# Two-layer diffusion backbone on one core: rows finished in whole pieces on VectorE, a gate applied at the PSUM exit, and a new order at the start of the experts

## The chip, the cores and the metric

The kernel runs on one core of a Trainium2 chip, with its engines TensorE (PE), VectorE (DVE), ScalarE (ACT), GpSimd (POOL) and SyncE (SP, which mostly issues DMAs). The metric is the device time of one execution in microseconds.

## The reference

512 latent tokens and 256 context tokens of width 1024 go through two layers. In layer 0 the mixer is neighbourhood attention beside grouped-query attention and all 768 tokens are carried on; in layer 1 it is a bidirectional RWKV-7 beside a bidirectional mLSTM, and only the 512 latent tokens leave it. After each mixer comes the same tail. What is computed there, cut to one stream:

```python
m = mixer(h)                                            # per layer
x = layer_norm(DN_ALPHA * x + g1 * (m @ mix_w_out[i]), ln_g[i, 0], ln_b[i, 0])
tokens = x * (1.0 + sc2) + sh2
scores = sigmoid(tokens @ router_w)
idx = top_k(scores + router_b, 6)                       # 6 of 64 experts
gates = 2.5 * scores[idx] / sum(scores[idx])
y = sum(gates * swiglu(tokens, w1[idx], w3[idx], w2[idx])) + swiglu(tokens, sw1, sw3, sw2)
x = layer_norm(DN_ALPHA * x + g2 * y, ln_g[i, 1], ln_b[i, 1])
```

`g1`, `sc2`, `sh2` and `g2` are vectors of 1024 that come from the conditioning; layer 0 has one set for the latent and one for the context tokens, layer 1 one set.

## The kernel before

**Tiles and stages.** Tokens lie in tiles of 128 rows by 1024 columns, six in layer 0 and four in layer 1. Each layer is a mixer (0 to 517 us of the profiled execution for attention, 1400 to 2160 for the recurrent one) and then `layer_tail`, which has four parts.

**First half of the tail.** `block` projects a tile (a product in fp32 is three matmuls of high and low parts, L414 to L416), leaves PSUM through DVE with the gate g1 (L1078) and adds the old row with its sum (L1079). `first_norm` then takes mean and variance in `spread` (ACT at L878 to L880, two short DVE operations at L881 and L882). It makes the router's input h by two DVE operations over the whole tile (L1087, L1088). The normalised row x itself, which stays in `x1` as the residual, is made by one ACT pass (L1089) and two POOL passes, times `ra` and plus `rb` (L1090, L1091). `route` works on the tile before: PE transposes h (L903), multiplies by the router (L955), ACT takes the sigmoid (L961), DVE finds the six experts and writes a 0/1 `mask` (L962 to L969), PE counts ranks with a triangular matrix (L973, L974), DVE makes `cat` (L976 to L979), PE turns it (L983).

**Start of the experts.** Ranks and gates are permuted on PE (L1166). `gates` (L932 to L936) splits the gates on DVE into bf16 parts `aux`. `slots` finds with DVE comparisons (`oh`, L1179) and small matmuls (L1184) which token sits in which slot of each unit. A unit is a set of up to 128 slots of one to four experts. `fetch` gathers the rows of a unit by an indirect DMA that POOL issues (L1207); `columns_of` turns them on PE (L1258) and leaves PSUM half by ACT and half by DVE (L1260, L1261).

**Experts.** For each unit: `up` (L1217), SwiGLU (ACT L1427, DVE L1432, transposes L1233), and `down`, whose result leaves PSUM in halves, by ACT (L1247) and DVE (L1248), as `ye`. POOL issues an indirect DMA that adds it to a DRAM buffer `acc` (L1249). Expert weights come as 1 MB thirds through a ring of ten buffers `ew`, loaded by SP (L998). 49 units run in layer 0 and 37 in layer 1. A shared expert is spread between them; its result is multiplied by g2 at the PSUM exit (L1311) and added to x by POOL (L1312). Bookkeeping for experts with more than 128 tokens (`ov`, `oc`, `blk`, L1363 to L1383) feeds a loop (L1386) that runs zero times with these inputs.

**Tail end.** `acc` is loaded back as two halves per tile (L1410). For each tile the halves are added (L1415) and multiplied by g2 (L1416), 512 columns on DVE and 512 on POOL; DVE adds the row to x with its sum (L1417); `spread` again; ACT normalises (L1419). In layer 0 `done` is `keep`, which stores the row. In layer 1 it is `store`: final gain and bias, 640 columns on DVE and 384 on POOL (L2417, L2418), and the output DMA (L2419).

**What sets the order.** The program is written in one sequence, and a scheduler that simulates engine times puts each engine's instructions in order before the run; `tc.issue_after(x)` keeps what is inside behind instruction x. A change in one operation's engine or length can therefore move others on all engines. Each engine then runs its own list in order.

Of the kernel before, what the change touches and what calls it, by code (L numbers as in the profile page):

```python
# [12 lines left out]
F32 = mybir.dt.float32  # L13
# [4 lines left out]
OP = mybir.AluOpType  # L18
# [337 lines left out]
class Kern:  # L356
# [530 lines left out]
    def layer_tail(self, layer, mT, x_rows, finish, part=None, done=None):  # L887
# [7 lines left out]
        with ExitStack() as es:  # L895
# [34 lines left out]
            def gates(dst, src, rest):  # L930
# [5 lines left out]
                nc.vector.tensor_copy(dst[:, :, :, 5], rest)  # L936
# [86 lines left out]
            with ExitStack() as es2:  # L1023
# [58 lines left out]
                def first_norm(t):  # L1082
# [6 lines left out]
                    nc.scalar.activation(x, x, AF.Identity, bias=both, scale=over)  # L1089
                    nc.gpsimd.tensor_tensor(x, x, ra, op=OP.mult)  # L1090
                    nc.gpsimd.tensor_tensor(x, x, rbb, op=OP.add)  # L1091
# [43 lines left out]
            def sort():  # L1135
# [33 lines left out]
                gates(aux, pq[:, :, 1], gq)  # L1169
# [68 lines left out]
            def down(hT, parts, ws, idx):  # L1238
# [8 lines left out]
                nc.scalar.copy(y[:, 0:512], py[:, 0:512])  # L1247
                nc.vector.tensor_copy(y[:, 512:], py[:, 512:])  # L1248
# [4 lines left out]
            def columns_of(xg):  # L1253
# [3 lines left out]
                for k in range(KT):  # L1257
                    nc.tensor.transpose(p[:, k], xg[:, k * 128:(k + 1) * 128], self.k_ident[:n, :n])  # L1258
                out = wp.tile([128, KT, 128], F32, name="xT", tag="xT", bufs=2)[:, :, :n]
                nc.scalar.copy(out[:, 0:4], p[:, 0:4])  # L1260
                nc.vector.tensor_copy(out[:, 4:8], p[:, 4:8])  # L1261
# [64 lines left out]
            while loaded < 5:  # L1326
                q, k = order[loaded]
                thirds[q, k], which[q] = routed_third(q, k)
                loaded += 1
            xgs[0] = fetch(slot_of(0)[0])  # L1330
            xgs[1] = fetch(slot_of(1)[0])
            sort()
            load()
            xgs[2] = fetch(slot_of(2)[0])
            xT = columns_of(xgs.pop(0))
            done_, begin = 0, 8
            for n, u in enumerate(units):
# [12 lines left out]
                if n == 6:  # L1350
# [32 lines left out]
            nc.vector.tensor_copy(blk[:, 128:129], cum[0:1, NE - 1:NE])  # L1383
            n_more = nc.values_load(blk[0:1, 128:129], min_val=0, max_val=127)
# [1055 lines left out]
```

## Time and profile before

| | us |
|---|---|
| median of 3 runs | 2927.14 (2916.27 to 2935.19) |
| profiled execution, its own time | 2924.99 |
| its span, first to last instruction | 2923.0 |
| PE busy | 2418.9 (83%) |
| DVE busy | 1214.3 (42%) |
| ACT busy | 737.1 (25%) |
| POOL busy | 760.8 (26%) |
| mean granted TensorE clock | 0.898 |

The shares are means over stages with different limits: PE is busy nearly throughout the experts and idle in the two tail ends. So the stages are read one by one. A group of instructions is told by its line; DVE's idle time before a group, and what ended it, says which engine it waited for. A bracket in a timeline, as [3.01 <-DVE mask L969], is the idle time of that engine just before the instruction, and what ended it.

### The profile page before, as it was taken

The numbers are of one execution on the slowest core, as the hardware profiler recorded it, in microseconds if no ns is written. First come the engines' busy times: TensorE is split into PE (matmuls) and PEld (weight loads), VectorE is DVE, ScalarE is ACT, GpSimd is POOL, SyncE is SP. The second block draws the span as 40 slices with busy tenths as digits, with TensorE's granted clock in tenths as the row PEclk, the third lists the DMA queues.
The fourth block names the chain that finished last, engine by engine and source line by source line (L and its number), as shares of the span: only waits on it lengthen the run. The fifth ranks groups of instructions, "written<-read, shape, count | busy, mean of one in ns | idle before, by whom it ended". The sixth has DMA issues, their size and how long they took to land. (4 is left out here: it accounts for less than half of the span.)

```text
span 2923.0 us, 45988 instructions
## 1 busy us (share of the span) xinstructions
PE 2418.9 (83%) x18007; PEld 1469.8 (50%) x18007; DVE 1214.3 (42%) x2595; ACT 737.1 (25%) x1605; POOL 760.8 (26%) x674
## 2 busy tenths in 40 slices
PE   7789895969989999994799778866866988979981
PEld 6658664854434444331578666756755333324330
DVE  5742544473212222213753577856566212111114
ACT  3442443231101111111554443413222101111102
POOL 0111011121112222214344354434622111111114
PEclk9899997879999999997899787879976999999995
DMA  8644445658999999996224445589635999999993
GB/s 315 213 127 124 111 132 99 236 199 313 377 343 327 359 332 347 378 343 197 86 71 111 132 126 153 145 238 299 241 129 214 383 378 354 358 393 353 353 378 115
DMA packets 254089, 722.31 MB, mean 247 GB/s; under 512 B 111096, under 2 KB 137464, under 8 KB 194736
## 3 DMA queue, kind: packets, MB, share of 16 engines
q1 hardware_dynamic: 216656, 631.86, 59.2%
q0 software_dynamic: 26560, 68.09, 9.3%
q10 hardware_dynamic: 10656, 19.40, 2.1%
q8 instruction: 143, 2.34, 0.4%
q14 instruction: 74, 0.61, 0.1%
HBM read 636.45 MB, written 107.33 MB: 254 GB/s over the span
## 5 line engine op out<-in xcount | busy, mean ns | idle before, releaser
L1217 PE MATMUL pb<-ew,xT 128*32 128x512 f32 (+2 forms) x3504 | 658.6, 605 | 24.4 <-DMA ew<-in_moe_w_dram 15.4
L1217 PEld LDWEIGHTS pb<-ew,xT 128*32 128x32 f32 (+2 forms) x3504 | 210.5, 127 | 397.3 <-issue 353.9
L1217 PE MATMUL pp<-ew,hT 128*32 128x512 f32 (+2 forms) x1752 | 327.2, 603 | 7.7 <-DMA ew<-in_moe_w_dram 5.2
L1432 DVE SCALAR_TENSOR_TENSOR hs<-s,gate,pb 128x256 f32<-128x256 f32 x86 | 41.3, 480 | 649.7 <-ACT s L1427 633.9
L1207 POOL DMA_INDIRECT xg<-rows,idx x86 | 88.8, 1032 | 649.4 <-PE pp L1258 276.0
L1427 ACT ACTIVATE s<-pb 128x256 f32<-128x256 f32 x96 | 36.1, 383 | 769.9 <-PE pb L1217 746.7
L1249 POOL DMA_INDIRECT acc<-ye,idx x86 | 137.0, 1593 | 323.9 <-DMA acc<-ye,idx 146.8
L1217 PEld LDWEIGHTS pp<-ew,hT 128*32 128x32 f32 (+2 forms) x1752 | 101.6, 126 | 189.1 <-issue 175.0
L414 PE MATMUL pp<-h_hi,w_hi 128*128 128x512 f32 (+1 forms) x432 | 162.5, 377 | 8.7 <-DVE mT L389 4.3
L415 PE MATMUL pp<-h_lo,w_hi 128*128 128x512 f32 (+1 forms) x432 | 159.7, 370 | 1.0 <-DVE h_lo L410 1.0
L416 PE MATMUL pp<-h_hi,w_lo 128*128 128x512 f32 (+1 forms) x432 | 159.7, 371 | 0.5 <-POOL w_lo L1570 0.5
L1570 POOL TENSOR_TENSOR w_lo<-w,w_hi 128x512 fp32r<-128x512 f32 x66 | 91.6, 1388 | 148.3 <-ACT w_hi L1569 127.9
L1258 PEld LDWEIGHTS pp<-consts,xg 128*128 128x128 f32 x688 | 79.5, 146 | 70.5 <-issue 47.4
L1258 PE MATMUL pp<-consts,xg 128*128 128x128 f32 x688 | 98.3, 288 | 14.4 <-DVE sh L1311 6.8
L1248 DVE COPY ye<-pp 128x512 f32<-128x512 f32 x86 | 59.1, 687 | 114.7 <-ACT ye L1247 109.6
L414 PE MATMUL pb<-w_hi,m_hi 128*128 128x256 f32 x256 | 77.9, 308 | 26.6 <-ACT w_hi L409 16.2
L414 PEld LDWEIGHTS pp<-h_hi,w_hi 128*128 128x128 f32 x432 | 86.9, 202 | 24.6 <-issue 6.8
L416 PEld LDWEIGHTS pp<-h_hi,w_lo 128*128 128x128 f32 x432 | 87.0, 202 | 16.4 <-issue 3.4
L440 PE MATMUL pb<-ada_w,cz 128*32 128x256 f32 x640 | 54.1, 456 | 49.6 <-DMA ada_w<-in_ada_w_dram 49.5
L1261 DVE COPY xT<-pp 128x512 f32<-128x512 f32 x86 | 59.4, 690 | 84.9 <-ACT xT L1260 84.9
L415 PEld LDWEIGHTS pp<-h_lo,w_hi 128*128 128x128 f32 x432 | 87.3, 202 | 14.1 <-issue 2.3
L1247 ACT COPY ye<-pp 128x512 f32<-128x512 f32 x86 | 50.4, 588 | 166.3 <-PE pp L1217 110.0
(515 smaller groups left out, 4737.5 us busy)
## 6 DMA issues: line engine op xcount, KB each, us to landing
ew<-in_moe_w_dram SPq DMA_DIRECT2D x384, 1024.0 KB
ada_w<-in_ada_w_dram SPq DMA_DIRECT2D x48, 1024.0 KB
w<-in_rec_w_dram ACTq DMA_DIRECT2D x66, 256.0 KB
steps<-dL SPq DMA_DIRECT2D x16, 1024.0 KB
acc<-zero SPq DMA_DIRECT2D x12, 1024.0 KB
ew<-acc SPq DMA_DIRECT2D x10, 1024.0 KB
w<-in_att_w_dram SPq DMA_DIRECT2D x18, 512.0 KB
cells<-dM SPq DMA_DIRECT2D x8, 1056.0 KB
```

The lines of the kernel that those rows point to most:

```text
L414: mm(out, l_hi, r_hi, start=start, stop=False)
L415: mm(out, l_hi, r_lo, start=False, stop=False)
L416: mm(out, l_lo, r_hi, start=False, stop=stop)
L440: nc.tensor.matmul(p[32 * g:32 * g + 32], self.cz[:, 4 * a + g, 30 - 2 * i:62 - 2 * i], w[:, 4 * a + g, :], start=i + a == 0, stop=i + 1 = ...
L1207: nc.gpsimd.indirect_dma_start(out=xg, out_offset=None, in_=self.rows[layer], in_offset=bass.IndirectOffsetOnAxis(ap=idx, axis=0), bounds_ ...
L1217: nc.tensor.matmul(out[s], x[:, s], ws[m], start=start, stop=stop, tile_position=(0, s.start))
L1247: nc.scalar.copy(y[:, 0:512], py[:, 0:512])
L1248: nc.vector.tensor_copy(y[:, 512:], py[:, 512:])
L1249: nc.gpsimd.indirect_dma_start(out=self.acc[layer], out_offset=bass.IndirectOffsetOnAxis(ap=idx, axis=0), in_=y, in_offset=None, bounds_ch ...
L1258: nc.tensor.transpose(p[:, k], xg[:, k * 128:(k + 1) * 128], self.k_ident[:n, :n])
L1261: nc.vector.tensor_copy(out[:, 4:8], p[:, 4:8])
L1570: nc.gpsimd.tensor_tensor(lo, w, hi.bitcast(F32), op=OP.subtract)
```

## The change

1. `first_norm`: x is finished by two DVE operations over the whole tile, (x + less) * ra and x * over + rb, in place of one ACT and two POOL passes (10 tiles in both layers).
2. `down` in layer 1: one DVE operation over 1024 columns, y = py * g2, in place of the two half copies; layer 0 is as before. The g2 row of layer 1 is therefore loaded before the first gather, and not at the seventh unit.
3. Start of the experts: the sequence is sort, load, transposes of unit 0, and only then the third gather, which is held behind the last of these transposes and the last operation of `gates`. The bookkeeping for full experts is held behind the last `xT` copy of the units.
4. `finish`, which in layer 1 loads the two rows fg and fb into ring buffers, is called before the last unit is closed and not after the loop.
5. Tail end: sums over whole rows on DVE (new L1421), times g2 only in layer 0 (new L1423), then the same sum with x (new L1424). `keep` does the ACT pass; `store` does two DVE operations over the whole row (new L2422, L2423) in place of ACT's pass and four half passes on DVE and POOL.

Counted over the whole program, POOL has 48 fewer compute instructions. ACT has 52 fewer passes and three more table loads: one more ahead of a Sqrt (L880) and one more ahead of a sigmoid (L961), both in layer 1's first norm, and one in the recurrent mixer.

```diff
@@ gates @@
-                nc.vector.tensor_copy(dst[:, :, :, 5], rest)
+                return nc.vector.tensor_copy(dst[:, :, :, 5], rest)
@@ first_norm @@
-                    nc.scalar.activation(x, x, AF.Identity, bias=both, scale=over)
-                    nc.gpsimd.tensor_tensor(x, x, ra, op=OP.mult)
-                    nc.gpsimd.tensor_tensor(x, x, rbb, op=OP.add)
+                    nc.vector.scalar_tensor_tensor(x, x, less, ra, op0=OP.add, op1=OP.mult)
+                    nc.vector.scalar_tensor_tensor(x, x, over, rbb, op0=OP.mult, op1=OP.add)
@@ down @@
-                nc.scalar.copy(y[:, 0:512], py[:, 0:512])
-                nc.vector.tensor_copy(y[:, 512:], py[:, 512:])
+                if layer:
+                    nc.vector.tensor_tensor(y, py, g2[0], op=OP.mult)
+                else:
+                    nc.scalar.copy(y[:, 0:512], py[:, 0:512])
+                    nc.vector.tensor_copy(y[:, 512:], py[:, 512:])
@@ columns_of: keeps its last transpose as .last and the DVE copy as .done @@
...
@@ start of the experts @@
+            if layer:
+                g2 = [self.row(wp, layer, "g20")]
             xgs[0] = fetch(slot_of(0)[0])
             xgs[1] = fetch(slot_of(1)[0])
-            sort()
+            sorted_ = sort()
             load()
-            xgs[2] = fetch(slot_of(2)[0])
             xT = columns_of(xgs.pop(0))
+            with tc.issue_after(columns_of.last.ins), tc.issue_after(sorted_.ins):
+                xgs[2] = fetch(slot_of(2)[0])
...
-                if n == 6:
+                if n == 6 and not layer:
...
+            fresh = lambda: wp.tile([128, 2048], F32, name="ew", tag="ew", bufs=RING)
+            done = finish(fresh)
             close(len(units) - 1)
             ov = wp.tile([128, 4, NE], F32, name="ov")
+            late = ExitStack()
+            late.enter_context(tc.issue_after(columns_of.done.ins))
...
@@ tail end @@
-                for eng, c in zip((nc.vector, nc.gpsimd), half):
-                    eng.tensor_tensor(y[:, c], y[:, c], more[:, c], op=OP.add)
-                    eng.tensor_tensor(y[:, c], y[:, c], g2[st[t]][:, c], op=OP.mult)
+                nc.vector.tensor_tensor(y, y, more, op=OP.add)
+                if not layer:
+                    nc.vector.tensor_tensor(y, y, g2[st[t]], op=OP.mult)
                 nc.vector.scalar_tensor_tensor(x, y, 1.0, x, op0=OP.mult, op1=OP.add, accum_out=sums[:, t:t + 1])
-                less, over, both = self.spread(wp, x, sums[:, t:t + 1], y)
-                nc.scalar.activation(x, x, AF.Identity, bias=both, scale=over)
-                done(t, x)
+                done(t, x, *self.spread(wp, x, sums[:, t:t + 1], y))
@@ store @@
-                for eng, c in ((nc.vector, slice(0, 640)), (nc.gpsimd, slice(640, D))):
-                    eng.tensor_tensor(x[:, c], x[:, c], gain[:, c], op=OP.mult)
-                    eng.tensor_tensor(x[:, c], x[:, c], offset[:, c], op=OP.add)
+                nc.vector.scalar_tensor_tensor(x, x, less, gain, op0=OP.add, op1=OP.mult)
+                nc.vector.scalar_tensor_tensor(x, x, over, offset, op0=OP.mult, op1=OP.add)
```

**Three places where engines' rows move.** In the changed kernel lines are numbered anew: L1183 is the old L1184, L1260 the old transposes L1258, L1263 the old `xT` copy L1261, L1178 the old L1179.

PE in layer 0's first norm, around the third tile, before (L414 to L416 project, L974 counts with the mask of the tile before, L903 turns the third tile's h):

```order
L414 MATMUL pb<-w_hi,m_hi 128x256
L974 LDWEIGHTS upper
L974 MATMUL pb<-mask,upper 128x64
L415 MATMUL pb<-w_lo,m_hi 128x256
L416 MATMUL pb<-w_hi,m_lo 128x256
L414 MATMUL pb<-w_hi,m_hi 128x256
L415 MATMUL pb<-w_lo,m_hi 128x256
L416 MATMUL pb<-w_hi,m_lo 128x256
L440 MATMUL pb<-ada_w,sw_4716 32x256 x8
L903 MATMUL pp<-consts,h_5370 128x128 x8
L449 MATMUL pb<-consts,sw_4716 128x128 x2
L955 MATMUL pb<-rw,hT 128x64 x8
```

and in the changed kernel:

```order
L414 MATMUL pb<-w_hi,m_hi 128x256
L415 MATMUL pb<-w_lo,m_hi 128x256
L416 MATMUL pb<-w_hi,m_lo 128x256
L903 MATMUL pp<-consts,h_5368 128x128 x8
L440 MATMUL pb<-ada_w,sw_4716 32x256 x8
L974 LDWEIGHTS upper
L974 MATMUL pb<-mask,upper 128x64
L449 MATMUL pb<-consts,sw_4716 128x128 x2
L955 MATMUL pb<-rw,hT 128x64 x8
```

The two rows that use the mask have moved from inside the projection to behind the transposes.

DVE at the same place, before (L1087 and L1088 make h; L962 to L969 make the mask of the tile before):

```order
L1087 SCALAR_TENSOR_TENSOR h_5370<-x_4671,rstd,G_4692 128x1024
L962 TENSOR_TENSOR bi<-sc,bias 128x64
L964 MAX top<-bi 128x8
L881 RECIPROCAL rstd<-rstd 128x1
L965 MEMSET top 128x2
L882 TENSOR_TENSOR rstd<-rstd 128x1
L1088 SCALAR_TENSOR_TENSOR h_5370<-h_5370,rstd,B_4696 128x1024
L966 MATCH_REPLACE rep<-top,bi 128x64
L968 TENSOR_TENSOR m<-rep,bi 128x64
L969 CAST mask<-m 128x128
L976 SCALAR_TENSOR_TENSOR cat,den<-sc,m 128x64
L977 RECIPROCAL den<-den 128x1
```

and in the changed kernel:

```order
L1087 SCALAR_TENSOR_TENSOR h_5368<-x_4671,rstd,G_4692 128x1024
L962 TENSOR_TENSOR bi<-sc,bias 128x64
L1089 SCALAR_TENSOR_TENSOR x_4671<-x_4671,rstd,ra 128x1024
L964 MAX top<-bi 128x8
L881 RECIPROCAL rstd<-rstd 128x1
L965 MEMSET top 128x2
L882 TENSOR_TENSOR rstd<-rstd 128x1
L1088 SCALAR_TENSOR_TENSOR h_5368<-h_5368,rstd,B_4696 128x1024
L1090 SCALAR_TENSOR_TENSOR x_4671<-x_4671,rstd,rb 128x1024
L966 MATCH_REPLACE rep<-top,bi 128x64
L968 TENSOR_TENSOR m<-rep,bi 128x64
L969 CAST mask<-m 128x128
```

The finishing of x now stands as two whole-tile rows (L1089, L1090) ahead of the mask's rows.

PE at the start of layer 0's experts, before (L1166 permutes, L1184 fills the sorted lists):

```order
L1158 MATMUL pb<-ye,consts 128x64
L1158 MATMUL pb<-ye,col 128x64
L1166 MATMUL pp<-ye,catT 128x128 x6
L1184 LDWEIGHTS oh
L1184 MATMUL pb<-aux,oh 128x6
```

and in the changed kernel:

```order
L1157 MATMUL pb<-ye,consts 128x64
L1157 MATMUL pb<-ye,col 128x64
L1165 MATMUL pp<-ye,catT 128x128 x6
L1260 MATMUL pp<-consts,xg 128x128 x8
L1183 LDWEIGHTS oh
L1183 MATMUL pb<-aux,oh 128x6
```

Eight transposes of the first unit now stand ahead of the sorted lists' matmuls.

DVE there, before (L932 stands three rows above the first row; `oh` rows are the comparisons for later units):

```order
L1179 TENSOR_TENSOR oh<-slot,rk 128x6x32
L1179 TENSOR_TENSOR oh<-slot,rk 128x6x96
L1179 TENSOR_TENSOR oh<-slot,rk 128x6x32
L1371 TENSOR_REDUCE oc<-ov 128x1
L933 TENSOR_TENSOR ye<-pp,aux 128x384
L1372 SCALAR_TENSOR_TENSOR ov,oc<-ov 128x64
L1373 TENSOR_SCALAR oc<-oc 128x1
L934 CAST aux<-ye 128x384
L1374 TENSOR_TENSOR oc<-consts,oc 128x1
L935 TENSOR_TENSOR ye<-ye,aux 128x384
L1375 TENSOR_SCALAR oc<-oc 128x1
L936 CAST aux<-ye 128x384
```

and in the changed kernel:

```order
L932 CAST aux<-pp 128x384
L933 TENSOR_TENSOR ye<-pp,aux 128x384
L934 CAST aux<-ye 128x384
L935 TENSOR_TENSOR ye<-ye,aux 128x384
L936 CAST aux<-ye 128x384
L1178 TENSOR_TENSOR oh<-slot,rk 128x768
L1178 TENSOR_TENSOR oh<-slot,rk 128x6x96
L1178 TENSOR_TENSOR oh<-slot,rk 128x6x32
L1178 TENSOR_TENSOR oh<-slot,rk 128x6x96
L1178 TENSOR_TENSOR oh<-slot,rk 128x6x32
L1178 TENSOR_TENSOR oh<-slot,rk 128x6x64 x2
L1263 COPY xT<-pp 128x512
```

The five rows of `gates` now follow each other, without comparisons and bookkeeping between them, and the copy `xT` follows the seventh comparison.

DVE at the end of layer 1, before:

```order
L1415 TENSOR_TENSOR ew<-ew 128x512
L1416 TENSOR_TENSOR ew<-ew,g_20243 128x512
L1417 SCALAR_TENSOR_TENSOR x_18794,sums<-ew,x_18794 128x1024
L1415 TENSOR_TENSOR ew<-ew 128x512
L1416 TENSOR_TENSOR ew<-ew,g_20243 128x512
L1417 SCALAR_TENSOR_TENSOR x_18794,sums<-ew,x_18794 128x1024
L881 RECIPROCAL rstd<-rstd 128x1
L1415 TENSOR_TENSOR ew<-ew 128x512
L882 TENSOR_TENSOR rstd<-rstd 128x1
```

and in the changed kernel:

```order
L1421 TENSOR_TENSOR ew<-ew 128x1024
L1424 SCALAR_TENSOR_TENSOR x_18776,sums<-ew,x_18776 128x1024
L1421 TENSOR_TENSOR ew<-ew 128x1024
L2422 SCALAR_TENSOR_TENSOR x_18776<-x_18776,rstd,ew 128x1024
L1424 SCALAR_TENSOR_TENSOR x_18776,sums<-ew,x_18776 128x1024
L881 RECIPROCAL rstd<-rstd 128x1
L1421 TENSOR_TENSOR ew<-ew 128x1024
L882 TENSOR_TENSOR rstd<-rstd 128x1
L2423 SCALAR_TENSOR_TENSOR x_18776<-x_18776,rstd,ew 128x1024
L1424 SCALAR_TENSOR_TENSOR x_18776,sums<-ew,x_18776 128x1024
```

Each tile has one sum, one sum with x and two finishing rows of 1024 columns each.

## Rows read from the trace of the kernel before

**Rows 1.** Stages (from:to, length, busy us and count by engine, PEclk, DMA share, GB/s).
```profile
517.00:645.00 128.00, 104.12 (x854) 93.18 (x852) 73.66 (x180) 41.13 (x68) 29.99 (x12) 0.87 0.52 198
645.00:1369.00 724.00, 683.76 (x4512) 279.12 (x4512) 174.46 (x408) 93.47 (x190) 142.97 (x104) 0.97 0.92 334
1400.00:2160.00 760.00, 610.62 (x5902) 510.01 (x5902) 487.76 (x922) 273.27 (x603) 351.24 (x348) 0.86 0.53 158
2240.00:2870.00 630.00, 547.12 (x3090) 210.23 (x3090) 120.73 (x317) 68.59 (x142) 104.80 (x77) 0.94 0.94 360
```

**Rows 2.** Waits of PE, 560 to 645 (us in total, times, longest).
```profile
PE pb L974 <- DVE mask L969: 8.3, 5, 3.0
```

**Rows 3.** Timeline, layer 0's first norm (start, us, engine, line, shape, [idle before <-releaser]).
```profile
594.56 2.34 POOL L1091 TENSOR_TENSOR x<-x,rb 128x1024 f32<-128x1024 f32 x1
594.60 2.38 DVE L969 CAST mask<-m 128x128 bf16<-128x128 f32 x1
597.04 0.19 PE L974 MATMUL pb<-mask,upper 128*128 128x64 bf16 x1 [3.01 <-DVE mask L969]
...
640.36 0.23 DVE L969 CAST mask<-m 128x128 bf16<-128x128 f32 x1
```

**Rows 4.** Groups of DVE, 517 to 645 (busy us, mean ns | idle before).
```profile
L1087 DVE SCALAR_TENSOR_TENSOR h<-x,rstd,G 128x1024 f32<-128x1024 f32 x6 | 7.7, 1284 | 2.9 <-ACT few L878 2.9
```

**Rows 5.** Timeline, start of layer 0's experts.
```profile
651.36 1.43 DVE L932 CAST aux<-pp 128x384 bf16<-128x384 f32 x1 [0.28 <-ACT rk L1168]
652.50 2.94 DVE L1179 TENSOR_TENSOR oh<-slot,rk 128x768 bf16<-128x768 bf16 x5
657.79 0.80 DVE L936 CAST aux<-ye 128x384 bf16<-128x384 f32 x1
662.64 1.53 PE L1217 MATMUL pb<-ew,xT 128*128 128x512 f32 x3
```

**Rows 6.** Timeline, layer 0's first norm, a table load on ACT.
```profile
629.95 1.28 ACT L961 ACT_TABLE_LOAD   x1
631.25 0.22 ACT L961 ACTIVATE sc<-pb 128x64 f32<-128x64 f32 x1
```

**Rows 7.** Timeline, layer 0's tail.
```profile
1363.89 3.30 SPq L1410 DMA_DIRECT2D ew<-acc  x6
1368.99 0.69 DVE L1415 TENSOR_TENSOR ew<-ew 128x512 f32<-128x512 f32 x1 [15.58 <-DMA ew<-acc]
...
1400.74 1.24 ACT L1419 ACTIVATE x<-x,rstd 128x1024 f32<-128x1024 f32 x1 [0.43 <-DVE rstd L882]
```

**Rows 8.** Waits of PE, 1400 to 2160, and (second row) 2160 to 2240.
```profile
PE pp L394 <- DVE ST L2132: 14.2, 3, 7.5
...
PE pb L974 <- DVE mask L969: 9.8, 4, 3.5
```

**Rows 9.** Waits of PE, 2240 to 2870.
```profile
PE pb L1217 <- DMA ew<-in_moe_w_dram: 15.4, 11, 3.0
```

**Rows 10.** Groups of DVE, 2240 to 2870.
```profile
L1248 DVE COPY ye<-pp 128x512 f32<-128x512 f32 x37 | 25.4, 687 | 43.9 <-ACT ye L1247 39.1 <-ACTq L1386 4.7
L1311 DVE TENSOR_TENSOR sh<-pp,g 128x1024 f32<-128x1024 f32 x4 | 4.9, 1225 | 20.2 <-PE pp L1308 14.6 <-issue 5.5
```

**Rows 11.** Groups of ACT, 2240 to 2870.
```profile
L1247 ACT COPY ye<-pp 128x512 f32<-128x512 f32 x37 | 21.7, 589 | 45.2 <-DMA acc<-ye,idx 30.3 <-PE pp L1217 14.8
```

**Rows 12.** Timeline, layer 1's tail.
```profile
2877.32 0.81 SPq L504 DMA_DIRECT2D ew<-vec  x2
2878.18 2.37 SPq L1410 DMA_DIRECT2D ew<-acc  x4
2885.72 0.69 DVE L1415 TENSOR_TENSOR ew<-ew 128x512 f32<-128x512 f32 x1 [18.73 <-DMA ew<-acc]
2899.55 1.23 DVE L1417 SCALAR_TENSOR_TENSOR x<-ew,x 128x1024 f32<-128x1024 f32 x1
2916.85 1.45 POOL L2418 TENSOR_TENSOR x<-x,ew 128x384 f32<-128x384 f32 x1
```

More of the change, by code (lines that the diff above doesn't have):

```diff
@@ L1168, in sort @@
                 nc.scalar.copy(rk, pq[:, :, 0])
-                gates(aux, pq[:, :, 1], gq)
+                return gates(aux, pq[:, :, 1], gq)
             def slots(members, at):
@@ L1257, in columns_of @@
                 for k in range(KT):
-                    nc.tensor.transpose(p[:, k], xg[:, k * 128:(k + 1) * 128], self.k_ident[:n, :n])
+                    columns_of.last = nc.tensor.transpose(p[:, k], xg[:, k * 128:(k + 1) * 128], self.k_ident[:n, :n])
                 out = wp.tile([128, KT, 128], F32, name="xT", tag="xT", bufs=2)[:, :, :n]
                 nc.scalar.copy(out[:, 0:4], p[:, 0:4])
-                nc.vector.tensor_copy(out[:, 4:8], p[:, 4:8])
+                columns_of.done = nc.vector.tensor_copy(out[:, 4:8], p[:, 4:8])
                 return out
@@ L1383, in layer_tail @@
             nc.vector.tensor_copy(blk[:, 128:129], cum[0:1, NE - 1:NE])
+            late.close()
             n_more = nc.values_load(blk[0:1, 128:129], min_val=0, max_val=127)
@@ L1400, in layer_tail @@
                 down(gated(up(xT, all_of, [w[0:2]]), gate[:, 0:1]), all_of, [w[2]], idx[:, 1])
-            fresh = lambda: wp.tile([128, 2048], F32, name="ew", tag="ew", bufs=RING)
-            done = finish(fresh)
             sums = wp.tile([128, nt], F32, name="sums")
-            half = slice(0, 512), slice(512, D)
             ys = {}
@@ L2388, in keep, with rows @@
         def keep(room):
-            def rows(t, x):
+            def rows(t, x, less, over, both):
+                nc.scalar.activation(x, x, AF.Identity, bias=both, scale=over)
                 if t < 4:
@@ L2413, in store, with rows @@
             gain, offset = (k.row(None, 1, v, out=w[:, n * D:n * D + D]) for n, v in enumerate(("fg", "fb")))
-            def rows(t, x):
-                for eng, c in ((nc.vector, slice(0, 640)), (nc.gpsimd, slice(640, D))):
-                    eng.tensor_tensor(x[:, c], x[:, c], gain[:, c], op=OP.mult)
-                    eng.tensor_tensor(x[:, c], x[:, c], offset[:, c], op=OP.add)
+            def rows(t, x, less, over, both):
+                nc.vector.scalar_tensor_tensor(x, x, less, gain, op0=OP.add, op1=OP.mult)
+                nc.vector.scalar_tensor_tensor(x, x, over, offset, op0=OP.mult, op1=OP.add)
                 nc.sync.dma_start(out[0, t * 128:(t + 1) * 128], x)
```

## The prediction

> **What bounds the kernel now.** I read the stages first [rows 1], because the kernel is not one thing. Layer 0's experts hold PE for 683.76 of 724 us: PE is the limit there, and what starts PE earlier is kept whole. Layer 1's experts hold PE for 547.12 of 630 us with the DMA share at 0.94, and PE waits there for weights in transit [rows 9]: what starts PE earlier is kept in part. In layer 0's first half (517 to 645 us) PE has 24 us idle, and DVE, busy 73.66 of 128 us, has 54. The recurrent mixer leaves PE 149 us idle in 760. In the two tail ends PE hardly works, and DVE and POOL finish rows.
>
> Then I read who is waited for. In the first half the longest waits of PE are for the mask: 8.3 us in layer 0 [rows 2], 9.8 us in layer 1 [rows 8]. The timeline shows why one of them is 3.01 us long: the cast that writes the mask took 2.38 us beside a POOL pass over a row that took 2.34, and the same cast took 0.23 us where POOL was quiet [rows 3]. So the POOL passes over x, though nobody waits for x, stretch short DVE operations for which PE waits.
>
> **The change, part by part.** All against the profiled execution: 2924.99 us, of which the span is 2923.0 and 2 us lie around it; it lies 2.2 us under the median of 2927.14.
>
> *First half, layer 0.* Twelve POOL passes and six ACT passes go; twelve DVE operations come. Their price is that of the nearest DVE operation of the same form and size, 1.284 us [rows 4], so 15.4 us of DVE. Cover: DVE's 54 idle us. One of each pair stands ahead of 1/std, where DVE waits for ACT anyway; the other stands ahead of the mask of the tile before. The mask's matmul has moved behind the transposes, so it has more time. The mask waits are 8.3 us; of these the last tile's, about 1.3, is a chain of short operations with no POOL beside it and stays; its cast is the last of [rows 3]. I take -7. If the 12 operations all displaced what PE waits for, it would be -8.3 + 15.4 = +7; if PE also loses other delays behind stretched operations, one more cast's stretch of 2.15 us in two tiles, -12. Between these I choose the waits, since the added rows stand where DVE was idle.
>
> *Start of the experts, layer 0.* The five operations of `gates` run from 651.36 to 658.59 with other work between [rows 5]. In a row they take at most 1.43 + 4 x 0.80 = 4.6, so they end at 656.0. Seven comparisons at 2.94 / 5 = 0.59 follow, 4.1, then the `xT` copy, priced as the copy of equal size, 0.69 [rows 10]: 660.8, and PE starts units some 0.1 us later, against 662.64. That is -1.7; the three middle operations are shorter than the last, so I take -2. Bounds: 0, if the gather of the first unit or ACT's half of `xT` becomes late next, and -3, if the middle operations and the comparisons together are 1.3 us shorter than I priced them. PE is the limit behind it, so it is kept.
>
> *Experts, layer 0.* Nothing else changes: 0.
>
> *Tail end, layer 0.* Work starts when `acc` has landed, at 1369.0, and ends with ACT's pass at 1401.98 [rows 7]. Now DVE does six rows alone: a sum and a product at 1.22 each (the two-operand DVE pass over 1024 columns [rows 10], its source in PSUM) and the sum with x at 1.23, which is its time without POOL [rows 12]: 6 x 3.67 = 22.0. I allow 0.5 us a tile for short operations between, and 4 for the statistics and ACT's pass after the last sum: 1369.0 + 29 = 1398, -4. Bounds 0 and -7.
>
> *Recurrent mixer.* No operation in it is changed, but its order is, since the scheduler's times moved. Nothing prices this; a single wait of PE on a DVE result reached 7.5 us there [rows 8], so 0, bounded by -8 and +8.
>
> *First half, layer 1.* The mask waits of 9.8 us shrink by about 4 (the longest, 3.5, is of the kind of [rows 3]; the others I count as mostly chain). Against that ACT loads tables twice more, each 1.28 us [rows 6], ahead of the last tiles' statistics: 2.6. I take -1.5, bounds -6 and +3 (no wait gone, loads paid). The row shows the next ACT pass 0.02 us after the load's end. The Trainium skill (ScalarE: Activation LUTs, What ACT_TABLE_LOAD costs) adds a drain of about 1380 ns to the 1283 ns of a load; the trace has the same load and no drain behind it, and with the page's 2.66 us the stage would come out 2.8 us later and the whole at 2897.
>
> *Experts, layer 1.* The start gains by the same means on four tiles' data instead of six: -1.3, and as PE waits for weights there anyway [rows 9] I count -1. The g2 row (0.5 MB broadcast to 128 rows) leaves a stream that moves 360 GB/s [rows 1]: at most 1.4, I count -1. `down`'s exit: ACT's half takes 0.589 [rows 11] and DVE's half 0.687; DVE waits 39.1 us for ACT in all [rows 10], so the halves come one after the other: 1.28. One DVE operation on 1024 columns from PSUM times a row takes 1.225 [rows 10]. 37 x 0.05 = -2 at most, off PE's path: 0. Bounds for the stage: -7 and +5.
>
> *Tail end, layer 1.* Two row loads stand ahead of `acc` on SP's queue at 2877.32; `acc` is issued at 2878.18 and the first tile works at 2885.72 [rows 12]. They now go out before the last unit is closed. So `acc` is issued at 2877.32 and lands as in layer 0, 5.1 us later [rows 7]: 2882.4, -3.3. From there DVE alone: per tile a sum at 1.22, the sum with x at 1.23 and two finishing rows at 1.284, 5.02; four tiles 20.1, and 1.9 for short operations and one stall at the end: 22.0, so 2904.4. Before, POOL ended at 2918.3 [rows 12]. That is -13.9. g2's product is gone from this place, paid at the PSUM exit. Bounds: -9, if row loads or ACT's statistics hold DVE, and -16.
>
> Sum: -7 -2 -4 +0 -1.5 -1 -1 -13.9 = -30.4. Predicted: 2925 - 30.4 = 2894.6, 2894 rounded.
>
> **The rivals.**
>
> *Only the tail ends keep their gain.* DVE in the first halves, now carrying x, is as late as POOL made it, or layer 1's expert stage swallows what comes earlier. For it: 25.7 us of DVE are added in the first halves (20 x 1.284). Against it: DVE is idle by 54 us in the first of them. Then -18: 2907.
>
> *The PSUM exit on one engine is slower.* If the two half copies really ran side by side, an exit took 0.69 and now takes 1.225, and where PSUM holds up PE, 37 x 0.54 = 20 us are lost: 2894.6 + 20 = 2915. Against it: DVE's idle time before its half ends with ACT's half [rows 10]. The Trainium skill (PSUM — Partial Sum Buffer, Specifications (TRN2)) says that ScalarE and VectorE can read PSUM in parallel at full bandwidth while they use different banks, and speaks so against this edit. The trace shows them in turn here, whatever the hardware would allow.
>
> *The reordered mixer is slower.* Place: the in-order DVE queue of the recurrent mixer. A DVE result that PE awaits is now listed behind one that waits for another engine. Price: 7.5 us for each such wait [rows 8]. Five of them, 37 us, eat the gain and put the kernel at 2932, slower than before; eight would pass 1% slower. For it: PE has 149 us of idle time there already, so its queues are delicate. Against it: none of its operations changed.
>
> *The start gains nothing.* The comparisons of later units stand ahead of `xT`, so the transposes were moved for nothing, in both layers: 2897.6.
>
> **How the numbers follow.** The forecast gets 0.55, only the tails 0.20, the exit 0.08, the mixer 0.10, no gain at the start 0.07. One per cent, about what a measurement of this kernel can tell from no change, is 29 us: the line is 2898. The forecast's own bounds, taken one or two at a time, run from 2876 to 2904, and I give 0.47 of its 0.55 to below 2898, and 0.04 of the last rival's 0.07. So faster 0.51; slower by over 1% only the worst of the mixer's case, 0.05; within 1% the rest, 0.44. The range 2874 to 2917 holds the forecast with its bounds, the tails alone and the exit; outside it lie the mixer's case and the ends, under 0.2.
>
> **What would show it.** In the first halves the mask's cast takes 0.23 us in each tile, and PE's waits for it nearly vanish; units start 2 us after where they would by 660.8; the last ACT pass of layer 0 ends about 29 us after `acc` lands; layer 1's last DVE row ends about 22 us after `acc`, and POOL has no compute left in either tail end. A DVE `ye` row of 1.225 with PE waiting for PSUM behind it would show the exit rival. A stage from 1400 on longer than 768 us would make the prediction wrong through the mixer, and a first half in layer 0 not shorter than 128 us through DVE's added 15.4.

## The result, and the profile after

The changed kernel took 2886.26 us (median of 4 runs, 2875.97 to 2891.72) against 2921.70 us for the kernel before (4 runs, the three known and 2915.5). The ratio of the runs is 0.9859, 95% interval 0.9831 to 0.9887: 1.4% faster, or 33 to 49 us. The forecast was 2894, 1.1% under its profiled execution.

The two traces differ by more, 2923.0 against 2873.8 us of span. So I cut both at the same events and compare pieces. First the changed kernel, columns as in [rows 1]: from the first transpose of h in layer 0 to the first count matmul of the sort; to the first unit's product; from the issue of the `acc` loads to the end of the last ACT pass; the recurrent mixer with the start of layer 1's first half; layer 1's units; layer 1's rows.

```profile
562.50:632.72 70.22, 56.20 (x455) 50.20 (x455) 49.05 (x154) 25.49 (x50) 1.12 (x1) 0.81 0.53 198
632.72:645.45 12.73, 8.37 (x62) 7.40 (x63) 8.45 (x15) 1.27 (x3) 1.02 (x1) 0.50 1.00 402
1340.31:1373.39 33.08, 3.44 (x10) 1.66 (x10) 22.09 (x36) 18.54 (x37) 0.00 (x0) 0.50 0.63 227
1373.39:2160.60 787.21, 627.49 (x6008) 525.49 (x6008) 503.17 (x952) 283.68 (x619) 355.93 (x348) 0.86 0.52 159
2218.31:2844.18 625.87, 543.51 (x3038) 206.36 (x3038) 132.97 (x295) 48.33 (x102) 104.18 (x76) 0.94 0.94 356
2849.52:2870.13 20.61, 0.00 (x0) 0.00 (x0) 19.76 (x28) 8.61 (x21) 0.00 (x0) 0.50 0.51 207
```

The same pieces in the kernel before:

```profile
565.65:646.87 81.22, 59.10 (x455) 51.34 (x455) 55.71 (x144) 32.52 (x56) 31.11 (x13) 0.78 0.46 175
646.87:662.64 15.77, 7.93 (x63) 7.49 (x63) 13.12 (x40) 1.28 (x3) 1.99 (x2) 0.50 0.99 382
1363.89:1401.98 38.09, 3.44 (x10) 1.65 (x10) 26.95 (x36) 18.74 (x37) 20.88 (x12) 0.50 0.55 197
1401.98:2189.40 787.42, 627.72 (x6008) 525.68 (x6008) 504.60 (x951) 281.49 (x618) 351.44 (x348) 0.86 0.53 159
2253.79:2878.18 624.39, 540.62 (x3032) 204.12 (x3030) 109.56 (x269) 67.42 (x139) 103.74 (x76) 0.95 0.93 355
2885.72:2918.30 32.58, 0.00 (x0) 0.00 (x0) 28.82 (x32) 13.21 (x25) 26.00 (x16) 0.50 0.32 129
```

| piece | before | changed | difference | forecast |
|---|---|---|---|---|
| all up to the first transpose of h | 565.65 | 562.50 | -3.2 | 0 |
| layer 0, first half | 81.2 | 70.2 | -11.0 | -7 |
| layer 0, start of the experts | 15.8 | 12.7 | -3.0 | -2 |
| layer 0, experts | 701.2 | 694.9 | -6.4 | 0 |
| layer 0, tail end | 38.1 | 33.1 | -5.0 | -4 |
| recurrent mixer | 787.4 | 787.2 | -0.2 | 0 |
| layer 1, first half | 52.0 | 46.5 | -5.5 | -1.5 |
| layer 1, start of the experts | 12.4 | 11.2 | -1.2 | -1 |
| layer 1, experts | 624.4 | 625.9 | +1.5 | -1 |
| layer 1, loads and rows, end | 44.8 | 29.6 | -15.2 | -13.9 |

Two differences stand where the change alters no operation on PE: -3.2 ahead of it and -6.4 in layer 0's experts. The second is mostly this execution's: four experiments below with the same order there took 699.2 to 700.4 us. Without the two the trace gives about -39.6, inside the interval of the ratio.

In layer 0's first half of the changed kernel, the mask's cast and PE's wait for it (durations are least, median and most in ns; the wait is total, times):

```profile
L969 DVE CAST mask<-m x6: 226/226/227, 571.3 to 626.1; 128x128 bf16<-128x128 f32 x6
  PE pb L974: 1.8, 3
```

All six casts take 0.23 us, and PE's wait has fallen from 8.3 to 1.8 us. Nothing stretches them now, although DVE's own long operation stands close ahead (timeline of DVE, same place; answers to [rows 3]):

```profile
585.27 1.28 DVE L1090 SCALAR_TENSOR_TENSOR x<-x,rstd,rb 128x1024 f32<-128x1024 f32 x1
587.05 0.23 DVE L969 CAST mask<-m 128x128 bf16<-128x128 f32 x1
```

The start of layer 0's experts (timeline, answers to [rows 5]):

```profile
637.20 1.44 DVE L932 CAST aux<-pp 128x384 bf16<-128x384 f32 x1 [3.02 <-ACT rk L1167]
640.90 0.80 DVE L936 CAST aux<-ye 128x384 bf16<-128x384 f32 x1
641.41 3.87 DVE L1178 TENSOR_TENSOR oh<-slot,rk 128x768 bf16<-128x768 bf16 x7
643.72 1.97 PE L1260 MATMUL pp<-consts,xg 128*128 128x128 f32 x8
645.20 0.69 DVE L1263 COPY xT<-pp 128x512 f32<-128x512 f32 x1
645.48 1.48 PE L1216 MATMUL pb<-ew,xT 128*128 128x512 f32 x2
```

`gates` runs through in 4.5 us instead of 7.2, the seven comparisons take 3.87 and the copy follows at once.

Layer 0's tail end (answers to [rows 7]): the loads land after 5.1 us as before, and the last pass ends 28.0 us later instead of 33.0.

```profile
1340.31 3.38 SPq L1417 DMA_DIRECT2D ew<-acc  x6
1345.40 1.23 DVE L1421 TENSOR_TENSOR ew<-ew 128x1024 f32<-128x1024 f32 x1 [17.50 <-DMA ew<-acc]
1372.15 1.24 ACT L2395 ACTIVATE x<-x,rstd 128x1024 f32<-128x1024 f32 x1 [0.43 <-DVE rstd L882]
```

Layer 1's end (answers to [rows 12]):

```profile
2844.18 2.18 SPq L1417 DMA_DIRECT2D ew<-acc  x4
2849.52 1.22 DVE L1421 TENSOR_TENSOR ew<-ew 128x1024 f32<-128x1024 f32 x1 [15.56 <-DMA ew<-acc]
2868.85 1.28 DVE L2423 SCALAR_TENSOR_TENSOR x<-x,rstd,ew 128x1024 f32<-128x1024 f32 x1
```

The loads land 5.3 us after their issue (7.5 before), and DVE is through 20.6 us later, where DVE and POOL together took 32.6.

### The profile page after: what moved, and what is told of

Its sections match the earlier page's. It is cut to its first block, busy times and chain, and to the rows that moved or that the text cites. A ratio compares the mean times of both kernels' runs of the same rounds, so it can differ in the third digit from the quotient of the medians.

```text
span 2873.8 us, 45879 instructions
## 1 busy us (share of the span) xinstructions
PE 2405.8 (84%) x18007; PEld 1462.8 (51%) x18007; DVE 1209.9 (42%) x2611; ACT 706.4 (25%) x1557; POOL 668.7 (23%) x626
## 3 DMA queue, kind: packets, MB, share of 16 engines
q8 instruction: 143, 2.34, 0.3%
## 5 line engine op out<-in xcount | busy, mean ns | idle before, releaser
L414 PE MATMUL pp<-h_hi,w_hi 128*128 128x512 f32 (+1 forms) x432 | 160.1, 372 | 5.0 <-DVE mT L389 4.3
L416 PE MATMUL pp<-h_hi,w_lo 128*128 128x512 f32 (+1 forms) x432 | 157.7, 366 | 0.6 <-POOL w_lo L1575 0.6
L1260 PEld LDWEIGHTS pp<-consts,xg 128*128 128x128 f32 x688 | 79.5, 146 | 78.2 <-issue 53.7
L1260 PE MATMUL pp<-consts,xg 128*128 128x128 f32 x688 | 98.6, 288 | 21.4 <-DVE sh L1313 6.5
L1263 DVE COPY xT<-pp 128x512 f32<-128x512 f32 x86 | 59.3, 690 | 97.8 <-ACT xT L1262 97.8
L414 PE MATMUL pb<-w_hi,m_hi 128*128 128x256 f32 x256 | 77.8, 307 | 26.5 <-ACT w_hi L409 15.6
L440 PE MATMUL pb<-ada_w,cz 128*32 128x256 f32 x640 | 54.3, 457 | 50.3 <-DMA ada_w<-in_ada_w_dram 50.2
L414 PEld LDWEIGHTS pp<-h_hi,w_hi 128*128 128x128 f32 x432 | 85.5, 198 | 21.1 <-DVE mT L389 4.4
L416 PEld LDWEIGHTS pp<-h_hi,w_lo 128*128 128x128 f32 x432 | 84.9, 197 | 15.8 <-issue 3.1
L1262 ACT COPY xT<-pp 128x512 f32<-128x512 f32 x86 | 50.3, 585 | 157.2 <-PE pp L1260 156.0
L415 PE MATMUL pb<-w_lo,m_hi 128*128 128x256 f32 x256 | 76.5, 301 | 1.5 <-DVE w_lo L410 1.5
```

Of the source, the lines that this page charges most:

```text
L414: mm(out, l_hi, r_hi, start=start, stop=False)
L415: mm(out, l_hi, r_lo, start=False, stop=False)
L416: mm(out, l_lo, r_hi, start=False, stop=stop)
L440: nc.tensor.matmul(p[32 * g:32 * g + 32], self.cz[:, 4 * a + g, 30 - 2 * i:62 - 2 * i], w[:, 4 * a + g, :], start=i + a == 0, stop=i + 1 = ...
L1260: columns_of.last = nc.tensor.transpose(p[:, k], xg[:, k * 128:(k + 1) * 128], self.k_ident[:n, :n])
L1263: columns_of.done = nc.vector.tensor_copy(out[:, 4:8], p[:, 4:8])
```

## The experiments

Each kernel is cut at the same events; pieces in us, one execution each, ratio against the kernel before on the same chip. The chip of e1 to e4 gave the kernel before 2945.64 us, that of e5 to e8 2947.27, that of e9 to e12 2944.46; ratios and pieces can be compared, absolute times cannot.

| | first half 0 | start 0 | mixer | first half 1 | experts 1 | landing | rows 1 | ratio (95%) |
|---|---|---|---|---|---|---|---|---|
| before | 81.2 | 15.8 | 787.4 | 52.0 | 624.4 | 7.5 | 32.6 | 1 |
| changed | 70.2 | 12.7 | 787.2 | 46.5 | 625.9 | 5.3 | 20.6 | 0.9859 (0.9831 to 0.9887) |
| e1_norm_only | 70.1 | 15.8 | 793.7 | 45.2 | 625.3 | 7.5 | 32.6 | 0.9955 (0.9937 to 0.9973) |
| e2_no_pool_l1 | 81.5 | 15.8 | 787.1 | 42.6 | 621.7 | 7.7 | 32.6 | 0.9975 (0.9952 to 0.9998) |
| e3_halves | 70.4 | 12.8 | 788.3 | 46.5 | 623.1 | 5.3 | 24.5 | 0.9851 (0.9828 to 0.9874) |
| e4_old_start | 70.6 | 15.8 | 800.6 | 45.7 | 622.2 | 5.3 | 20.6 | 0.9884 (0.9848 to 0.9920) |
| e5_late_rows | 70.4 | 12.8 | 788.1 | 46.8 | 625.7 | 7.6 | 20.6 | 0.9862 (0.9820 to 0.9905) |
| e6_split_x | 70.1 | 11.0 | 793.1 | 45.5 | 612.6 | 5.3 | 20.6 | 0.9813 (0.9776 to 0.9850) |
| e7_split_y | 70.5 | 12.8 | 789.5 | 45.7 | 610.6 | 5.2 | 24.5 | 0.9814 (0.9775 to 0.9853) |
| e8_up_first | 70.1 | 7.6 | 787.7 | 45.5 | 626.8 | 5.2 | 20.6 | 0.9855 (0.9823 to 0.9888) |
| e9_x_serial | 70.2 | 11.1 | 791.3 | 45.2 | 611.1 | 5.0 | 20.6 | 0.9797 (0.9766 to 0.9828) |
| e10_y_banks | 70.6 | 12.8 | 791.4 | 46.8 | 610.0 | 5.3 | 20.6 | 0.9820 (0.9785 to 0.9855) |
| e11_best | 71.0 | 8.5 | 791.5 | 46.9 | 608.3 | 5.2 | 20.6 | 0.9776 (0.9749 to 0.9803) |
| e12_best_y | 70.4 | 8.5 | 794.0 | 45.6 | 611.5 | 5.2 | 20.6 | 0.9785 (0.9754 to 0.9816) |

Layer 0's experts took 694.8 to 702.8 us in all of them, with no pattern that follows the edits. e3_halves, e5_late_rows, e7_split_y and e10_y_banks have the changed kernel's order up to layer 1's experts on PE and DVE, but for two neighbouring rows of 14969 on PE. In these five the recurrent mixer took 787.2 to 791.4 us and layer 0's experts 694.8 to 700.4: such pieces differ by 4 to 6 us from execution to execution. The attention mixer at the start differs by more. Its rows on PE stand in one order in all fourteen kernels, and in the twelve experiments it took 579.6 to 601.5 us.

**e1_norm_only**: the kernel before with this alone:

```diff
-                    nc.scalar.activation(x, x, AF.Identity, bias=both, scale=over)
-                    nc.gpsimd.tensor_tensor(x, x, ra, op=OP.mult)
-                    nc.gpsimd.tensor_tensor(x, x, rbb, op=OP.add)
+                    nc.vector.scalar_tensor_tensor(x, x, less, ra, op0=OP.add, op1=OP.mult)
+                    nc.vector.scalar_tensor_tensor(x, x, over, rbb, op0=OP.mult, op1=OP.add)
```

> The kernel before with the first norm's x finished on DVE, and nothing else. Theory (POOL's passes stretched the short DVE operations, DVE does the added ones in idle time): layer 0's first half from the first transpose of h to the count matmuls 11 us shorter, PE's wait for the mask there from 8.3 to about 2; layer 1's first half 4 us shorter; layer 0's expert stage unchanged within 3; in all -12 to -18. Rival (the shorter first half of the changed kernel comes from the other edits, or from a kinder clock in that execution): the first halves shrink by less than 5 us together.

The first halves came out at 70.1 and 45.2, the whole of the changed kernel's gain there. The rival falls. Layer 0's expert stage took 4.9 us less, where no more than 3 was expected, and the mixer, which no edit touches, 6.3 us more.

**e2_no_pool_l1**: `if layer == 0:` ahead of the two POOL passes.

> The kernel before, with the two POOL passes over x left out in layer 1 only (its output then lacks the gain and offset of the first norm in the residual). Nothing is added on DVE, and ACT's pass stays. Theory: PE's wait for the mask in layer 1's first half falls from 9.8 to about 1.5, as in the changed kernel (1.4), and the half is 4 to 6 us shorter, so DVE's eight added operations cost at most 2 us. Rival (DVE's added operations and the table loads eat most of the gain): the half is 8 us shorter or more without them.

PE's wait for the mask in layer 1's first half:

```profile
PE pb L974 <- DVE mask L969: 1.4, 1, 1.4
```

The wait fell as in the changed kernel, but the half was 9.4 us shorter than before, not 4 to 6: the rival's number. Of what leaving out the POOL passes is worth in layer 1, the changed kernel realises 5.5. The other 3.9 go where DVE and ACT do more; 2.6 of them are the two table loads that the changed kernel has there (ACT's groups, 2130 to 2207 us):

```profile
L961 ACT ACT_TABLE_LOAD x3 | 3.8, 1283 | 0.1
L880 ACT ACT_TABLE_LOAD x2 | 2.6, 1283 | 0.0
```

Before there were two and one. In the changed kernel's last tile one of each stands between ACT's statistics and the root, on which DVE's h and PE's transposes wait (timeline):

```profile
2187.14 1.15 ACT L879 ACTIVATE junk<-x,rstd 128x1024 bf16<-128x1024 f32 x1
2188.40 1.28 ACT L961 ACT_TABLE_LOAD   x1
2189.93 1.28 ACT L880 ACT_TABLE_LOAD   x1
2191.23 0.29 ACT L880 ACTIVATE rstd<-rstd,eps 128x1 f32<-128x1 f32 x1
2193.16 1.97 PE L903 MATMUL pp<-consts,h 128*128 128x128 f32 x8 [2.23 <-DVE h L1088]
```

The root comes 4.1 us after the statistics begin, against 1.3 in e2_no_pool_l1. e1_norm_only, with the same DVE operations and loads in another order, lost 2.5 in all.

**e3_halves**: the product with g2 back in the tail, the exit in halves, in layer 1.

```diff
-                if layer:
-                    nc.vector.tensor_tensor(y, py, g2[0], op=OP.mult)
-                else:
...
-                if not layer:
-                    nc.vector.tensor_tensor(y, y, g2[st[t]], op=OP.mult)
+                nc.vector.tensor_tensor(y, y, g2[st[t]], op=OP.mult)
```

> The changed kernel, but in layer 1 the expert result leaves PSUM in halves by ACT and DVE as before, and the product with g2 stands in the tail as one whole-row DVE operation per tile. Theory (halves come one after the other, 1.28 against 1.225 us, off PE's path): layer 1's expert stage within 3 us of the changed kernel's 626; the tail end 4.9 us longer (4 x 1.22); in all +5 against the changed kernel. Rival (one engine's exit is slower than two): the expert stage 10 to 20 us shorter and the whole 5 to 15 us faster than the changed kernel.

The stage differs by 2.8 us, within what one program scatters; the rows take 3.9 more. The whole is not told apart from the changed kernel; the +5 that was expected does not show in the ratio. So, by the pieces, the edit at the exit is worth the tail's 3.9 us and nothing else that shows.

**e4_old_start**: the old order of the third gather and the transposes, no hold on the bookkeeping.

> The changed kernel with the old start of the experts: third gather ahead of the transposes, no hold on the bookkeeping. Theory: in layer 0 the first unit starts 2 to 3 us later behind the permuting matmuls (15.8 us after their start instead of 12.8), in layer 1 about 1 us later; +3 to +4 in all. Rival (the transposes gain nothing, since the comparisons stand ahead of the copy anyway, or the gather is late): no difference above 1 us in either layer.

The start is back at 15.8 and 11.9, so the new order is worth 3.0 and 0.7 us. The ratio does not tell the whole apart from the changed kernel. In the profiled execution the mixer took 13.4 us more:

```profile
1418.40:2219.00 800.60, 634.92 (x6009) 531.86 (x6009) 505.06 (x952) 279.26 (x617) 351.78 (x348) 0.84 0.52 156
```

PE is busier there by 7.4 us at a granted clock of 0.84 against 0.86, and idles for 6 us more. The mixer's operations are the same and their order is not, but the execution was a long one from its start: it is the longest of the run's four (2930.32 us; the others 2901.63 to 2918.06). The attention mixer, with the same order on PE, took 601.5 us in it against 582.4 to 583.0 in the other three experiments on that chip. Before the first transpose of h, PE waited longer there for the conditioning weights (e1_norm_only, then e4_old_start):

```profile
PE pb L440 <- DMA ada_w<-in_ada_w_dram: 61.7, 14, 11.5
PE pb L440 <- DMA ada_w<-in_ada_w_dram: 79.5, 18, 11.3
```

How much of the 13.4 is the order's stays open.

**e5_late_rows**: `finish(fresh)` behind the loop again.

> The changed kernel with the rows fg and fb loaded behind the loop again, as before. Theory: the sums' loads are issued 0.9 us later and land 7.5 instead of 5.3 us after, so the whole is 3 us longer and every other stage as it was, since no order ahead of the last unit moves. Rival (the loads land late for another reason, the last scatters): no difference, landing still 5.3 us.

```profile
2876.30 1.03 SPq L504 DMA_DIRECT2D ew<-vec  x2
2877.38 2.25 SPq L1417 DMA_DIRECT2D ew<-acc  x4
2884.98 1.23 DVE L1421 TENSOR_TENSOR ew<-ew 128x1024 f32<-128x1024 f32 x1 [19.24 <-DMA ew<-acc]
```

The landing took 7.6 us after the issue, 2.3 more, and the issue came 1.1 after that of the first row's load. The rival falls. The order ahead stayed as expected, but for the two neighbouring rows in the mixer, and no piece there changed by more than 4.4 us. The ratio does not show the 3 us.

**e6_split_x, e7_split_y, e9_x_serial, e10_y_banks**: what the PSUM exits cost. In e6_split_x:

```diff
-                p = self.pair((128, KT, 128))[:, :, :n]
+                pa, pb_ = (self.bank((128, 4, 128))[:, :, :n] for _ in range(2))
...
-                nc.scalar.copy(out[:, 0:4], p[:, 0:4])
-                columns_of.done = nc.vector.tensor_copy(out[:, 4:8], p[:, 4:8])
+                nc.scalar.copy(oa, pa)
+                columns_of.done = nc.vector.tensor_copy(ob, pb_)
```

> The changed kernel with the transposed rows of a unit in two PSUM banks and two SBUF tiles in place of one pair and one tile, so that ACT's and DVE's halves wait for PE only and may run side by side. Theory (in the kernel before the second half waits because both read one PSUM tile; PE seldom waits for it): the halves overlap at 0.59 and 0.69 us each, and the time is within 6 us of the changed kernel's. Rival A (two engines reading PSUM at once slow each other): each half takes 1 us or more. Rival B (the serial exit held up PE): the expert stages lose 10 us or more.

> As e3_halves (product with g2 in the tail), with the expert result of layer 1 in two PSUM banks, so that the two half copies can run side by side. Theory (the exit is off PE's path): layer 1's expert stage as in e3_halves, 623 us, within 4; rows at the end 24.5 us. Rival (a side-by-side exit of 0.69 is worth what one engine's 1.225 loses, 37 x 0.54 us): the stage 15 to 20 us shorter.

In the changed kernel the two halves of a unit's rows follow each other (timeline, layer 1):

```profile
2315.00 0.59 ACT L1262 COPY xT<-pp 128x512 f32<-128x512 f32 x1 [4.12 <-PE pp L1260]
2315.62 0.69 DVE L1263 COPY xT<-pp 128x512 f32<-128x512 f32 x1
```

In e6_split_x they overlap:

```profile
2308.65 0.58 ACT L1263 COPY xTa<-pb 128x512 f32<-128x512 f32 x1 [5.64 <-PE pb L1260]
2309.03 0.69 DVE L1264 COPY xTb<-pb 128x512 f32<-128x512 f32 x1 [0.48 <-PE pb L1260]
```

They overlap by 0.20 us and take the same 0.58 and 0.69 us: rival A falls. The Trainium skill (PSUM — Partial Sum Buffer, Specifications (TRN2)) says that both engines read PSUM in parallel at full bandwidth on different banks; the trace agrees. But layer 1's experts took 612.6 instead of 625.9 us, so rival B's number came out for layer 1, and the whole is by ratio some 14 us under the changed kernel's, where at most 6 were expected (the intervals overlap). e7_split_y, with its results in single banks, took 610.6 where e3_halves took 623.1. Layer 0's experts gained nothing (702.8 us). Either the overlap was worth this, or the banks. e9_x_serial gives both halves to ACT (`nc.scalar.copy(ob, pb_)`); e10_y_banks keeps the transposes in a pair and puts the result in two banks, both times g2 on DVE:

> As e6_split_x (transposed rows in two PSUM banks), but both halves leave by ACT, one after the other, 2 x 0.585 us, so the exit is as serial as in the changed kernel. Theory 1 (what shortened layer 1's experts by 13 us was that the two halves run side by side): the stage is back at 623 to 626 us. Theory 2 (it was that the transposes no longer hold one of the two PSUM pairs, so that the expert results never wait for a pair): the stage stays near 613 us.

> The changed kernel with the expert result of layer 1 in two PSUM banks, both times g2 by DVE, 0.69 us each and one after the other; the transposes stay in a pair. Theory 1 (side by side is what counts): layer 1's experts at 623 to 626 us, as the changed kernel. Theory 2 (the pairs were short): near 611 us, as e7_split_y, with the rows at the end at 20.6 and not 24.5.

Groups of ACT in e9_x_serial, and its layer 1 experts as one piece:

```profile
L1264 ACT COPY xTb<-pb 128x512 f32<-128x512 f32 x36 | 21.3, 591 | 14.6 <-PE pb L1260 14.5
L1263 ACT COPY xTa<-pb 128x512 f32<-128x512 f32 x36 | 21.1, 586 | 100.0 <-PE pb L1260 97.6 <-PE pb L1183 2.2
```

```profile
2243.60:2854.70 611.10, 541.60 (x3050) 200.00 (x3038) 107.53 (x243) 67.46 (x139) 103.85 (x76) 0.96 0.96 365
```

Both halves on one engine, one after the other, and the stage is as short: theory 1 falls. Four kernels take either the transposes or the results out of the two PSUM pairs, and all four gain 12 to 16 us, whether the halves overlap or not. In the changed kernel PE waits for a pair to be emptied (waits of PE in layer 1's experts):

```profile
PE pp L1310 <- DVE ye L1247: 4.9, 3, 2.5
PE pp L1260 <- DVE ye L1247: 4.2, 3, 1.9
```

By theory 2 the results' pairs would no longer hold up PE once the transposes have left them. In e6_split_x they still do:

```profile
PE pp L903 <- DVE ye L1247: 9.4, 2, 7.0
PE pp L1216 <- DVE ye L1247: 3.3, 4, 1.4
```

PE's waits for `ye` in a pair are 13.4 us there and 8.9 in e9_x_serial, against 9.3 in the changed kernel. What went in both are the waits of the units' transposes for a pair (12.4 us in all) and the product's waits for the copies `xT` (6.7). In e7_split_y and e10_y_banks no wait for `ye` in a pair is left, but about 6 us for a bank that holds it. So, by PE's waits, theory 2 is borne out in part.

Two more things changed in all four. A half in a bank of its own can leave before the other half is written: in e6_split_x and e9_x_serial alike the second copy ends 0.73 us after a unit's last transpose, against 1.35 in the changed kernel (medians of 37 units). So e9_x_serial's halves left in turn, but not as late as the changed kernel's. And the scheduler put PE's rows of the stage in another order, nearly one in e6_split_x and e9_x_serial, nearly another in e7_split_y and e10_y_banks. Which of the three shortens the stage is not shown: more pairs alone, or the banks in the old order, were not tried.

**e8_up_first, e11_best, e12_best_y.** In e8_up_first the first unit's product stands ahead of the sorted lists:

```diff
-            with tc.issue_after(columns_of.last.ins), tc.issue_after(sorted_.ins):
-                xgs[2] = fetch(slot_of(2)[0])
+            ph = up(xT, parts[0], [(thirds[q, 0], thirds[q, 1]) for q, a, r in units[0]])
+            with tc.issue_after(side_by_side.last.ins), tc.issue_after(sorted_.ins):
+                xgs[2] = fetch(slot_of(2)[0])
+                xgs[3] = fetch(slot_of(3)[0])
```

e11_best adds e6_split_x's banks in layer 1; e12_best_y adds e10_y_banks's.

> The changed kernel with the first unit's eight products, and not only its transposes, ahead of the sorted lists; the third and fourth gathers are held behind them. Theory (PE stands idle for 3.8 us for the comparisons of later units while the first unit's rows are ready at 639.4): layer 0's first unit starts 5 us earlier, layer 1's 1 us (its gather lands late there), and in all -3 to -6 if the recurrent mixer's order does not cost more. Rival (the gathers, issued later, are then what PE waits for): what is won at the start is lost at the third unit, and the whole is the same.

The start is 5.1 us shorter in layer 0 and unchanged in layer 1, where 1 us was expected, and the whole is not told apart from the changed kernel: a gain of that size is below what four runs resolve.

> e8_up_first with the transposed rows in two PSUM banks in layer 1 only, where that gained. If the two gains add: start of layer 0 7.6 us, layer 1's experts near 613, in all 15 to 18 us under the changed kernel, 1.9 to 2.1% under the kernel before, if the recurrent mixer's order costs nothing. Rival (the mixer's order costs up to 13 us, as in e4_old_start): no better than the changed kernel.

> e11_best with the expert result in two PSUM banks as well (as e10_y_banks). Theory 2 (the pairs were short, and are not once the transposes have left them): no gain over e11_best, or a loss of some us, since the four single banks now serve the transposes, the units' products and the results. Theory 1: no change either; a gain of 5 us or more would say that both exits held up PE.

Layer 1's experts and layer 0's start in e11_best:

```profile
2249.10:2857.30 608.20, 537.05 (x3071) 200.38 (x3070) 134.00 (x295) 48.99 (x102) 104.07 (x76) 0.96 0.96 367
661.80:670.30 8.50, 7.61 (x33) 6.88 (x33) 4.19 (x7) 1.28 (x3) 1.03 (x1) 0.50 0.99 366
```

Both gains add, the start's less 0.9 us. At 0.9776 (0.9749 to 0.9803) of the kernel before it has the lowest ratio, not told apart from e12_best_y (0.9785) and e9_x_serial (0.9797), and its interval lies below the changed kernel's. It is 0.0083 under the changed kernel's ratio, some 24 us, where 15 to 18 were expected; the intervals allow both. e12_best_y gained nothing more, which both theories allow, so it does not decide between them.

## Why the prediction was right, point by point

**First half, layer 0** (-7; measured -11.0). The mechanism was right: the cast fell from up to 2.4 us to 0.23, and e1_norm_only alone has the whole gain. The term was mis-sized. I took the mask waits less one chain; PE's waits for it did fall by 6.5 and its wait for the conditioning weights by 1.7 more (2.4 to 0.7). The rest is PE's work itself, which the sum left out: the same 455 matmuls kept it busy for 56.2 instead of 59.1 us, at a mean granted clock of 0.81 instead of 0.78 (in e1_norm_only 55.9 at 0.80, in e2_no_pool_l1, which leaves layer 0 as it was, 60.1 at 0.77). The 15.4 us of added DVE work cost nothing that shows in layer 0. The Trainium skill (SBUF — State Buffer, Who interferes with whom) calls the port pair that DVE shares with POOL an exclusive lock, which blocks the later one fully, and counts the cast among the operations that can take it; the cast of [rows 3] took 2.38 us beside a pass of 2.34, and 0.23 in all six tiles once the passes were gone, as that rule has it.

**Start, layer 0** (-2; -3.0) came out at its bound. `gates` took 4.5 and the comparisons 3.87, about as priced (4.6 and 4.1). But the sum let PE wait for the end of the `xT` copy, 0.69 us; PE began 0.28 us after that copy's start, right behind the second unit's transposes. **Tail end, layer 0** (-4; -5.0) was right.

**Mixer** (0, bounds 8 each way; -0.2). Right for this kernel. In the other runs the mixer took 787.1 to 794.0 us by order and execution, inside the bounds; only e4_old_start, in a long execution, lies outside with 13.4 us more. Whether an order alone can cost so much, as the slower rival has it, is not shown.

**First half, layer 1** (-1.5; -5.5). Mis-sized: I let less than half of the mask's waits go. They went from 9.8 to 1.4. The table loads cost about what I said, 2.6.

**Experts, layer 1** (-2 with the start; +0.3). For the exit the sum came out right, but the reason given, that it is off PE's path, failed: PE does wait for a pair that still holds `ye`, 9.3 us in the changed kernel and 10.5 before. The edit changes neither how long a pair is held (1.225 against 1.28 us) nor how many there are, so nothing came of it. The rival on the exit named the right place, but what it expected of two engines at once is not needed: with single banks the stage is 12 to 16 us shorter even where the halves leave in turn. The g2 row's 1 us does not show.

**Tail end, layer 1** (-13.9; -15.2). Right: -2.2 from the landing (I said -3.3, of which 0.9 was the earlier issue, ahead of the cut, and the loads land 0.2 later than in layer 0), -12.0 in the rows (DVE took 20.6, not 22.0), and 1.0 between the last row and the end, which I had not counted.

## What to carry to other kernels

An engine that nobody waits for can still be the slow one's cause: look for short operations whose duration changes tenfold, and at what ran beside them. Where two engines empty a PSUM tile, ask first how many such tiles there are and who queues for them; giving one user its own banks, with the earlier exit and the new order that came along, was worth 12 to 16 us here, the one-engine exit nothing. And a stage that an edit doesn't touch can move by more than the edit is worth, by its order or from one execution to the next. So compare pieces, not only the whole, and start with a piece that is the same in all kernels.

## What was not expected of the hardware

ACT and DVE read two PSUM banks at the same time, for 0.20 us of a copy, without slowing each other (0.58 and 0.69 us, alone or together). The same mixer instructions took 787 to 801 us by order and execution, with the granted clock at 0.86 and 0.84. And with one order on PE the attention mixer took 562.5 to 601.5 us, with PE's waits for the conditioning weights 50.2 us of it in the changed kernel and 79.5 in e4_old_start.
